# A two-layer encoder on one core: mean squares from token-major copies in the last layer, and activation halves made in two pieces

## The chip, the cores and the metric

The kernel runs on one core of one Trainium2 chip. The metric is the device time of one execution in microseconds (us), median of several runs. The engines are named as in the profile: PE is TensorE (matmuls; PEld its weight loads), DVE is VectorE, ACT is ScalarE, POOL is GpSimd, SP is SyncE, which issues most transfers. They run side by side, each in its own program order, and wait for one another by semaphores.

## The reference

512 tokens of width 1024 pass two layers in fp32. The first mixes tokens by stick-breaking attention with 16 heads, the second by a gated linear recurrence (rglru). Behind each mixer stands a squared-ReLU network of inner width 4096, and a norm ends the whole.

```python
def rms_norm(x, g):
    y = x * lax.rsqrt(jnp.mean(x * x, axis=-1, keepdims=True) + EPS)
    return y * g

def squared_relu_mlp(h, w1, w2):
    u = jax.nn.relu(h @ w1)
    return (u * u) @ w2

for layer in range(2):
    h = rms_norm(x, norm_mix[layer])
    x = x + (stick_breaking_attention(h, ...) if layer == 0 else rglru_block(h, ...))
    h = rms_norm(x, norm_mlp[layer])
    x = x + squared_relu_mlp(h, mlp_w1[layer], mlp_w2[layer])
return rms_norm(x, norm_final)
```

## The kernel before

Activations are held feature-major: 8 tiles `x[c]` of 128 features by 512 tokens. Every product is made three times over, with operands split into a high half (fp32r, a cast by ACT) and a low half (the remainder, a subtraction by DVE): high by high, high by low, low by high. So each weight slab of 128x1024 costs one cast `wh` on ACT and one subtraction `wl` on DVE, and PE multiplies with three passes.

The two networks (class `Mlp`) are computed in four quarters of the inner width. The first columns of the first matrix are plain products of 512 tokens (`product`, L236 to L238). All else is done with a 2x2 block scheme of seven products instead of eight. An "up" group takes seven products, P1 P5 P6 P3 P7 P2 P4, each of 24 matmuls of 256 columns (L1018), and gives activations `u[0]` to `u[3]`. Quarters two to four have two such groups (p = 0 and 1). The first quarter of the last layer has only group 1, since group 0 comes from four plain products. Then the "down" products of the second matrix follow, fourteen of 12 matmuls with 512 columns (L1149); their results are collected token-major in `mlp.c` (the program's names c, seen as `mlp.y(t, h)`: token tile t of 128, half h of the features).

Activations are ReLU and square, both on ACT (`u<-u`), with additions by DVE between them. Their halves for the second matrix stand in `bh` and `bl` for group 0 and in `sh` and `sl` for group 1; `split` makes them, sums of them (`sums`) follow in blocks 3 to 6. The additions on weights that the block scheme needs are made by DVE (`b<-b,b`) or by transfers that add, issued by POOL (L1094).

What order the work has: PE's order is as the program is written. Around the four quarters (`run`), ACT and DVE are `Ordered`: each instruction is told to follow the one recorded before it, so their queues stand as written, too. Each step of `run` calls `leave` for the step before: it copies or collects what that step left in PSUM, then prepares weights four steps on. Elsewhere a scheduler orders ACT, DVE and POOL by due times; SP's queue comes out of it as well.

The norm ahead of a network is applied behind it: the gain is multiplied in first, and each token's inverse mean square `rr` scales the token-major sums when they are collected (L797 with `ps,rr,c`). In the last layer `rr` comes from `Squares`: ACT squares the eight feature-major tiles (L159, L162), DVE adds them up (L164), PE sums over partitions by four products with ones (`inv_squares`, L174, of one column each), and DVE makes the inverse (L180 to L182). `transposed` has meanwhile copied `x` token-major into `mlp.c` (L1737, L1740), where the network's output is added.

At the end (`end`), DVE collects the last two products, ACT squares the tokens' rows with a running sum (`square`, L1764), `root` makes the factor, POOL multiplies some tiles with the last norm's gain ahead (`scaled`), and ACT (`one`, L1806) or DVE (`both`, L1797) scales the rows; SP stores them in the order of the program (L1788).

Of the kernel before, what the change touches and what calls it, by code (L numbers as in the profile page):

```python
# [64 lines left out]
def hybrid_encoder(  # L65
# [741 lines left out]
    class Mlp:  # L807
# [28 lines left out]
        def __init__(self, ctx, layer):  # L836
            self.layer, self.sq, self.first = layer, Squares(), None
            self.V, self.A = Ordered(V), Ordered(A)
            self.mp = ctx.enter_context(tc.tile_pool(name=f"mlp{layer}", bufs=2))
            self.c = [  # L840
                self.mp.tile([P, 2, S], F32, tag=f"c{i}", name=f"c{i}", bufs=1) for i in range(4)
            ]
            self.begun, self.a, self.next_slabs = set(), {}, []
            self.turns = count()
            self.blocks = ExitStack()
            self.bp = self.blocks.enter_context(tc.tile_pool(name=f"blocks{layer}", bufs=2))
            self.u, self.lows, self.s3, self.slots = {}, {}, [], None

            self.s41 = self.bp.tile([P, C // 2, S], F32R, tag="s41", name="s41", bufs=1)

        def y(self, t, h):
# [54 lines left out]
                    ]  # L906
            return self.a[p]

        def split(self, p, i, of, to):
            h, l = (t[:, i, to, :] for t in self.places(p))  # L910
            u = self.u[p][:, i, of, :]
            self.A.copy(h, u)
            self.ready = self.V.tensor_tensor(l, u, f(h), ALU.subtract)

        SUMS = (
            (2, 3, 2, ALU.subtract), (3, 0, 3, ALU.subtract), (0, 2, 0, ALU.subtract), (1, 0, 1, ALU.add),
# [242 lines left out]
        def run(self, first, between, end):  # L1159
# [102 lines left out]
            def leave(i):  # L1262

                if i < 0:
                    return
                kind, q4, p, name = steps[i]
                bank = sums[kind, q4, p if kind == "up" else 0][self.PRODUCTS[name][3]]
                if kind == "down":
# [39 lines left out]
                if later:  # L1308
                    later.pop()()
                prepare_or_hold(i)  # L1310
                if op:
                    def rest(u=u, at=at):
                        self.A.activation(u[at], u[at], AF.Relu)
                        self.square(u[at])
                        if p:
                            self.split_slot(p, u[at], at)

                    if p and name == "P3":
                        later.append(rest)
                    else:  # L1320
                        rest()
                    if name == "P2" and not p:
                        self.split(p, slice(0, 2), slice(0, 3), slice(0, 3))
                elif name == "P4" and p:
                    last_sums(u, self.SUMS[2:3])
                    self.split_slot(p, u[2], 5)
                    last_sums(u, self.SUMS[3:])
                    waiting[:] = [(p, u[j], 3 + j) for j in (0, 1, 3)]
                elif name == "P4":
                    self.sums(p, slice(0, 2), slice(1))  # L1330
                elif name in ("P5", "P6") and p:
                    n = ("P5", "P6").index(name)
                    if q4 + n == 0:
                        self.replace()
                    self.split(0, n, slice(0, 4), slice(3, 7))

            waiting, later, held = [], [], []
            if self.layer:
# [5 lines left out]
                self.halves_of_sums(0)  # L1344
                self.sums_of_x(2)
                self.halves_of_sums(1)
                for c in range(2):
                    self.squared(c, ps[c])
                make(0)
                add(1)  # L1350
                self.sums_of_x(3)
# [3 lines left out]
                self.halves_of_sums(3)  # L1355
                add(2)
                ps = self.product(3)
                self.rr = self.sq.inv_squares(bank("z"))
                self.squared(3, ps)
                self.split(0, slice(0, 2), slice(0, 3), slice(0, 3))  # L1360
                make(2)
                self.sums(0, slice(0, 2), slice(1))
                held.append(3)
# [32 lines left out]
                e.turn(False)  # L1396
            end([ws[len(steps) - 2 + g] for g in range(2)], sums["down", NQ - 1, 0]["X"])

        def blocks_from_the_third_slab(self, transposed, end):
            units = {("up", 0): self.from_up(0)}  # L1400

            def between():
# [5 lines left out]
                self.load(units["up", 0], (1, "b11"), (1, "b12"), (1, "b22"))  # L1408
                units["down", 0] = self.from_down(0)
                self.load(units["down", 0], (0, "b11"), (0, "b12"), (1, "b11"))  # L1410
                for n in range(C):
                    self.sq.chunk(n, x[n], e=V)
                return ps

            self.run(units, between, end)
# [311 lines left out]
    with ExitStack() as mctx:  # L1727
# [83 lines left out]
        def end(ws, xs):  # L1811
# [21 lines left out]
            for i, cols in enumerate(parts):  # L1833
                ps = mlp.bank()[:, :HS]
                for g in range(2):
                    mlp.times("P4", g, 1, ws[g], ps, True, cols)
                with tc.issue_after(scaled_two.ins) if i else nullcontext():
                    mlp.collect("P4", 1, ps, cols)
                sq = square(3, 0, 1 + i, cols, end=i == 1)
                if i == 0:  # L1840
                    scaled_two = both(2, 0, two)
                    one(2, 1, two, last=sq)
                    scaled(3, 0, cols, behind=mlp.y(2, 0))
            rt = root(3, 2)
            both(3, 0, rt, parts[1])
            one(3, 1, rt)
# [72 lines left out]
```

## Time and profile before

| | |
|---|---|
| median of 3 runs (lowest, highest) | 1025.52 us (1024.94, 1025.79) |
| profiled execution, its own time | 1025.03 us |
| its span, first to last instruction | 1022.8 us |
| mean granted TensorE clock | 0.998 |
| PE busy | 1014.2 us, 99% |
| DVE busy | 866.3 us, 85% |
| ACT busy | 708.9 us, 69% |
| POOL busy | 176.3 us, 17% |
| last layer's up and down products, and the end | from 726.3 us on |

Times in rows count from the start of the span. A row of the timeline has start, length, engine, line, operation, output and inputs, shapes, count, and in brackets how long the engine idled before it and what ended that. A row of groups has count, busy time and mean length in ns, then idle time ahead. L797 is a helper through which all `Ordered` instructions go, so such rows are told apart by their tiles. Matmuls overlap: successive starts tell their spacing, not their length.

### The profile page before, as it was taken

What the parts mean: (1) busy time and instruction counts of PE and PEld (TensorE: products, weight loads), DVE (VectorE), ACT (ScalarE), POOL (GpSimd) and SP (SyncE); (2) the same over time, 40 slices, a digit from 0 to 9 for tenths busy, and PEclk for the clock granted to TensorE, in tenths of its full rate; (3) what the DMA queues carried; (4) which work ended last, traced back from release to release, by engine and by line L of the source; (5) the groups of instructions that cost most, each with busy time, mean ns of one, the idle gap of its engine ahead of it and who ended that gap; (6) DMA issues with size and microseconds to landing.
All of it is one profiled execution on the core that took longest, in us unless ns stands there. A gap on an engine that the chain in (4) does not pass through costs nothing.

```text
span 1022.8 us, 16121 instructions
## 1 busy us (share of the span) xinstructions
PE 1014.2 (99%) x5962; PEld 893.6 (87%) x5962; DVE 866.3 (85%) x1159; ACT 708.9 (69%) x1094; POOL 176.3 (17%) x241
## 2 busy tenths in 40 slices
PE   9999999999999999999999999999999999999997
PEld 7988888888888988988988888888988988988986
DVE  7978787848789898898899888986898898898897
ACT  7777676836766863863875799966873763873865
POOL 0454444420010010010011121200010010010013
PEclk9999999999999999999999999999999999999999
DMA  7745454527536667667682575452467667667653
GB/s 238 237 105 147 126 148 100 161 94 290 137 78 200 179 146 203 170 144 204 175 209 81 149 189 157 104 206 83 97 138 202 165 144 201 174 142 203 173 114 106
DMA packets 53550, 161.53 MB, mean 158 GB/s; under 512 B 6752, under 2 KB 8288, under 8 KB 53472
## 3 DMA queue, kind: packets, MB, share of 16 engines
q1 hardware_dynamic: 42240, 120.48, 35.6%
q0 software_dynamic: 10944, 39.85, 22.8%
q8 instruction: 47, 0.77, 0.3%
q14 instruction: 31, 0.25, 0.1%
q10 hardware_dynamic: 288, 0.18, 0.1%
HBM read 138.46 MB, written 4.19 MB: 139 GB/s over the span
## 4 chain that ended last, share of the span: by engine, by line
PE 94%; DVE 3%; ACT 2%; DMA 1%; issue 1%; SPq 0%; DVEq 0%; ACTq 0%
PE ps_t L1149 16%; PE ps_acc L1018 9%; PE ps_acc L1149 8%; PE ps_z L1018 8%; PE ps_acc L236 5%; PE ps_acc L238 5%; PE ps_acc L237 5%; PE ps_o L1018 5%; PE ps_z L1149 4%; PE ps_t L236 2%; PE ps_t L237 2%; PE ps_t L238 2%; PE ps_t L636 2%; PE ps_o L236 2%; PE ps_o L237 2%; PE ps_o L238 2%
## 5 line engine op out<-in xcount | busy, mean ns | idle before, releaser
L797 ACT CAST wh<-b 128x1024 fp32r<-128x1024 f32 x174 | 180.6, 1050 | 119.8 <-DVE b L797 81.0
L797 DVE TENSOR_TENSOR wl<-b,wh 128x1024 fp32r<-128x1024 f32 x174 | 210.3, 1218 | 39.9 <-ACT wh L797 38.4
L1094 POOL DMA_DIRECT2D b<-in_w_dn x40 | 34.9, 873 | 292.8 <-DVE b L797 196.7
L236 PE MATMUL ps_acc<-xgh,wh 128*128 128x512 f32 x192 | 78.3, 408 | 0.0
L238 PE MATMUL ps_acc<-xgl,wh 128*128 128x512 f32 x192 | 75.2, 391 | 0.0
L237 PE MATMUL ps_acc<-xgh,wl 128*128 128x512 f32 x192 | 75.1, 391 | 0.0
L1094 POOL DMA_DIRECT2D b<-in_w_up x26 | 22.6, 869 | 297.2 <-DMA b<-in_w_up 80.9
L797 ACT ACTIVATE u<-u 128x512 f32<-128x512 f32 x103 | 65.0, 632 | 12.3 <-DVE u L797 10.4
L614 DVE TENSOR_TENSOR_SCAN scan<-keep,later 128x128 f32<-128x128 f32 (+1 forms) x64 | 58.2, 913 | 16.4 <-ACT keep L604 10.4
L618 POOL TENSOR_TENSOR w<-w,scan 128x128 f32<-128x128 f32 (+1 forms) x64 | 53.4, 836 | 55.4 <-DVE scan L614 50.2
L797 DVE TENSOR_TENSOR b<-b,b 128x1024 f32<-128x1024 f32 x50 | 61.1, 1222 | 1.3
L231 DVE TENSOR_TENSOR wl<-raw,wh 128x512 fp32r<-128x512 f32 (+2 forms) x66 | 57.1, 893 | 5.6 <-ACT wh L229 5.6
L229 ACT CAST wh<-raw 128x512 fp32r<-128x512 f32 (+2 forms) x66 | 46.5, 742 | 21.3 <-PE ps_acc L238 7.3
L797 DVE TENSOR_TENSOR u<-u 128x512 f32<-128x512 f32 (+1 forms) x85 | 54.2, 638 | 4.1 <-ACT u L797 2.3
L797 ACT CAST wh<-raw 128x1024 fp32r<-128x1024 f32 x47 | 49.0, 1048 | 3.2 <-PE ps_acc L1149 3.1
L1018 PE MATMUL ps_z<-xgh,wh 128*128 128x256 f32 x216 | 50.7, 277 | 0.0
L1149 PE MATMUL ps_t<-wh,sl 128*128 128x512 f32 x120 | 46.9, 391 | 0.2 <-DVE sl L797 0.2
L1149 PE MATMUL ps_t<-wh,bl 128*128 128x512 f32 x120 | 46.8, 390 | 0.0
L1149 PE MATMUL ps_t<-wh,sh 128*128 128x512 f32 x120 | 46.8, 390 | 0.0
L1149 PE MATMUL ps_t<-wh,bh 128*128 128x512 f32 x120 | 46.8, 390 | 0.0
L797 DVE TENSOR_TENSOR wl<-raw,wh 128x1024 fp32r<-128x1024 f32 x37 | 45.5, 1229 | 1.1 <-ACT wh L797 1.1
L1018 PE MATMUL ps_acc<-low,wh 128*128 128x256 f32 x192 | 44.7, 276 | 0.0
(423 smaller groups left out, 3209.9 us busy)
## 6 DMA issues: line engine op xcount, KB each, us to landing
b<-in_w_dn SPq DMA_DIRECT2D x48, 512.0 KB, 4.1
b<-in_w_dn POOLq DMA_DIRECT2D x40, 512.0 KB, 5.5
b<-in_w_up SPq DMA_DIRECT2D x39, 512.0 KB, 4.4
b<-in_w_up POOLq DMA_DIRECT2D x26, 512.0 KB, 5.4
raw<-in_w_dn SPq DMA_DIRECT2D x16, 512.0 KB, 4.5
raw<-in_w_in SPq DMA_DIRECT2D x16, 512.0 KB, 3.7
raw<-in_w_up SPq DMA_DIRECT2D x13, 512.0 KB, 4.2
raw<-in_w_qk SPq DMA_DIRECT2D x12, 512.0 KB, 3.8
```

What stands on the lines that cost most here:

```text
L229: A.copy(wh[:, k, :], raw[:, k, :])
L231: V.tensor_tensor(wl[:, k, :], raw[:, k, :], f(wh[:, k, :]), ALU.subtract)
L236: PE.matmul(ps, wh, ah, start=start, stop=False)
L237: PE.matmul(ps, wl, ah, start=False, stop=False)
L238: PE.matmul(ps, wh, al, start=False, stop=stop)
L614: V.tensor_tensor_scan(sc[:, S - n : S][:, ::-1], keep[:, :n][:, ::-1], later[:, S - n :][:, ::-1], 1.0, ALU.mult, ALU.max,)
L618: G.tensor_tensor(wt, wt, sc[:, S - n + 1 : S + 1], ALU.mult)
L636: PE.transpose(tr[:, (qb - kb) * P : (qb - kb + 1) * P], w[pair, j, qb][:, kb * P : (kb + 1) * P], ident,)
L797: ins = getattr(self.e, name)(*args, **kwargs)
L1018: PE.matmul(ps[:, i * HS : (i + 1) * HS], m, y, start=new and i == k == low == 0 and y is h, stop=(low, i, k) == steps[-1], skip_group_che ...
L1094: G.dma_start(out=unit[b].rearrange("p j n -> p (j n)"), in_=unit["src"](to), accum_op=ALU.add)
L1149: PE.matmul(sums[to][i], m, y[:, j, :], start=new and g == j == low == 0 and m is h, stop=g == low == j == 1, skip_group_check=not new,)
```

## The change

1. In the last layer the eight feature-major squares, their sum, the four products with ones and DVE's three small operations go. Instead ACT squares the eight token-major tiles `mlp.y(t, h)` with an accumulator (`squares_of_tokens`): two tiles behind `halves_of_sums(1)`, two behind the fourth plain product (both pairs with a PSUM bank for the unused output), one each behind the first and the fourth up product, two behind the second down product (unused output in SBUF). There `inv_squares_of_tokens` makes `rr` with POOL, DVE (reciprocal) and POOL. The old `leave` is renamed `left`, and a new `leave` calls it first.
2. In the last layer's first quarter, the halves of group 0 are made in two pieces: for i = 0 behind the first two plain products, for i = 1 behind the fourth.
3. In quarters two to four of both layers, the halves of group 0's `u[1]` and `u[2]` are made ahead (high halves behind P7, low halves behind P2's addition) and those of `u[0]` alone behind P2.
4. At the end the collection of tile (3, 0)'s second half no longer stands behind the scaling of tile (2, 0): that scaling now follows the last collection, and POOL's last product with the gain does not wait for it either.

```diff
+            self.ss = spare[:, 8:].rearrange("p (h t) -> p h t", h=2)
...
-        def split(self, p, i, of, to):
+        def split(self, *which):
+            self.high_halves(*which)
+            self.low_halves(*which)
+
+        def high_halves(self, p, i, of, to):
+            self.A.copy(self.places(p)[0][:, i, to, :], self.u[p][:, i, of, :])
+
+        def low_halves(self, p, i, of, to):
             h, l = (t[:, i, to, :] for t in self.places(p))
-            u = self.u[p][:, i, of, :]
-            self.A.copy(h, u)
-            self.ready = self.V.tensor_tensor(l, u, f(h), ALU.subtract)
+            self.ready = self.V.tensor_tensor(l, self.u[p][:, i, of, :], f(h), ALU.subtract)
...
+                left(i)
+                if self.layer and i < 10 and place(i) in (7, 10, 15):
+                    ts = {7: ((2, 0),), 10: ((3, 0),), 15: ((2, 1), (3, 1))}[place(i)]
+                    junk = home.tile([P, S], F32, tag="osum", name="junk", bufs=1)
+                    self.squares_of_tokens(junk, *ts)
+                    if place(i) == 15:
+                        self.inv_squares_of_tokens()
...
                 prepare_or_hold(i)
+                if name == "P2" and not p:
+                    self.low_halves(0, slice(0, 2), slice(1, 3), slice(1, 3))
...
+                    if name == "P7" and not p:
+                        self.high_halves(0, slice(0, 2), slice(1, 3), slice(1, 3))
                     if name == "P2" and not p:
-                        self.split(p, slice(0, 2), slice(0, 3), slice(0, 3))
+                        self.split(p, slice(0, 2), slice(0, 1), slice(0, 1))
...
                 self.halves_of_sums(1)
+                self.squares_of_tokens(bank("t"), (0, 0), (1, 0))
                 for c in range(2):
                     self.squared(c, ps[c])
+                self.split(0, 0, slice(0, 3), slice(0, 3))
                 make(0)
...
                 ps = self.product(3)
-                self.rr = self.sq.inv_squares(bank("z"))
+                self.squares_of_tokens(bank("t"), (0, 1), (1, 1))
                 self.squared(3, ps)
-                self.split(0, slice(0, 2), slice(0, 3), slice(0, 3))
+                self.split(0, 1, slice(0, 3), slice(0, 3))
...
+        def squares_of_tokens(self, junk, *tiles):
+            for t, h in tiles:
+                self.A.activation(
+                    junk, self.y(t, h), AF.Square, accum_out=self.ss[:, h, t : t + 1]
+                )
+
+        def inv_squares_of_tokens(self):
+            rr = self.rr = small.tile([P, 2 * NB], F32, tag="rr", name="rr")
+            G.tensor_tensor(rr[:, :NB], self.ss[:, 0, :], self.ss[:, 1, :], ALU.add)
+            G.tensor_scalar(rr[:, :NB], rr[:, :NB], 1.0 / D, EPS, ALU.mult, ALU.add)
+            self.V.reciprocal(rr[:, :NB], rr[:, :NB])
+            G.tensor_scalar(rr[:, NB:], rr[:, :NB], -1.0, None, ALU.mult)
...
-                for n in range(C):
-                    self.sq.chunk(n, x[n], e=V)
...
-                with tc.issue_after(scaled_two.ins) if i else nullcontext():
-                    mlp.collect("P4", 1, ps, cols)
+                mlp.collect("P4", 1, ps, cols)
                 sq = square(3, 0, 1 + i, cols, end=i == 1)
                 if i == 0:
-                    scaled_two = both(2, 0, two)
                     one(2, 1, two, last=sq)
-                    scaled(3, 0, cols, behind=mlp.y(2, 0))
+                    scaled(3, 0, cols)
+            both(2, 0, two, last=mlp.gained)
```

How this stands in the engines' queues, at three places. First ACT around the fourth plain product of the last layer (`u<-ps_acc` takes that product, `bh<-u` are the halves of group 0, `wh` weights), before:

```order
L797 CAST s_7404<-x 128x512
L797 ACTIVATE u<-ps_acc 128x512
L797 ACTIVATE u<-u 128x512
L797 CAST bh<-u 128x2x768
L797 CAST wh<-b_7531 128x1024
L797 COPY u<-ps_z 128x512
L797 CAST wh<-b_7535 128x1024
```

and now:

```order
L797 CAST s_7410<-x 128x512
L797 ACTIVATE ps_t,eps_t<-c_7404 128x512 x2
L797 ACTIVATE u<-ps_acc 128x512
L797 ACTIVATE u<-u 128x512
L797 CAST bh<-u 128x768
L797 CAST wh<-b_7537 128x1024
L797 COPY u<-ps_z 128x512
L797 CAST wh<-b_7541 128x1024
L797 ACTIVATE junk,eps_t<-c_7405 128x512
```

Two squares stand ahead of the fourth product's activation, half of the split has left this place (it stands ahead of the first up weights now), and one square follows the second of the weights.

Second, ACT in the second quarter of the last layer, around P2 of group 0, before:

```order
L797 ACTIVATE u<-u 128x2x256 x2
L797 CAST wh<-b_8120 128x1024
L797 ACTIVATE u<-u 128x2x256 x2
L797 CAST bh<-u 128x2x768
L797 ACTIVATE u<-ps_acc 128x2x256
L797 ACTIVATE u<-u 128x2x256
L797 COPY u<-ps_z 128x512
L797 CAST wh<-b_8176 128x1024
```

and now:

```order
L797 ACTIVATE u<-u 128x2x256 x2
L797 CAST bh<-u 128x2x512
L797 CAST wh<-b_8114 128x1024
L797 ACTIVATE u<-u 128x2x256 x2
L797 CAST bh<-u 128x2x256
L797 ACTIVATE u<-ps_acc 128x2x256
L797 ACTIVATE u<-u 128x2x256
L797 COPY u<-ps_z 128x512
L797 CAST wh<-b_8170 128x1024
```

Two thirds of the halves have moved ahead of a weight's cast and of P2's activation; one third stands where all stood. On DVE the two low halves, of 1024 and 512 elements, stand together where the one of 1536 stood, behind the weight's subtraction.

Third, DVE at the end (the products `ps_o` and `ps_t` of 256 columns are the two last collections, `c_7399` and later `c_7405` tiles 2 and 3 of half 0), before:

```order
L797 SCALAR_TENSOR_TENSOR c_7399<-ps_o,rr,c_7399 128x256
L1784 RECIPROCAL rt<-rt 128x1
L1797 SCALAR_TENSOR_TENSOR c_7399<-c_7399,rt,gb 128x512
L797 SCALAR_TENSOR_TENSOR c_7399<-ps_t,rr,c_7399 128x256
L1784 RECIPROCAL rt<-rt 128x1
L1797 SCALAR_TENSOR_TENSOR c_7399<-c_7399,rt,gb 128x256
```

and now:

```order
L797 SCALAR_TENSOR_TENSOR c_7405<-ps_o,rr,c_7405 128x256
L1818 RECIPROCAL rt<-rt 128x1
L797 SCALAR_TENSOR_TENSOR c_7405<-ps_t,rr,c_7405 128x256
L1831 SCALAR_TENSOR_TENSOR c_7405<-c_7405,rt,gb 128x512
L1818 RECIPROCAL rt<-rt 128x1
L1831 SCALAR_TENSOR_TENSOR c_7405<-c_7405,rt,gb 128x256
```

The last collection and the scaling of 512 columns have changed places. SP's stores keep their order: tile (2, 0), (2, 1), then the three of tile 3.

Between the last layer's two weight subtractions and the first collection, DVE's queue has the new reciprocal; in POOL's queue the addition and the scaling for the mean stand together ahead of a transfer that adds, and the negation behind it.

More of the change, by code (lines that the diff above doesn't have):

```diff
@@ L1265, in leave, with left @@
                     return
+                left(i)
[5 more added lines that the diff above has]
+                        self.inv_squares_of_tokens()
+            def left(i):
                 kind, q4, p, name = steps[i]
```

## The prediction

> **What bounds the kernel now.** I read the page's busy row and its chain of waits first, then TensorE's own waits, then stage by stage how long equal work takes.
>
> ```profile
> span 1022.8 us, 16121 instructions
> PE 1014.2 (99%) x5962; PEld 893.6 (87%) x5962; DVE 866.3 (85%) x1159; ACT 708.9 (69%) x1094; POOL 176.3 (17%) x241
> PE 94%; DVE 3%; ACT 2%; DMA 1%; issue 1%; SPq 0%; DVEq 0%; ACTq 0%
> PE ps_t L1149 <- DVE sl L797: 0.2, 1, 0.2
> ```
>
> TensorE (PE) bounds it: 94% of the chain that ends last, and apart from its start only one recorded wait, 0.2 us. What can be won is therefore small and of three kinds: matmuls that disappear, matmuls spaced wider than elsewhere, and the tail after PE. The last two do not show as waits; they show as equal work that takes unequal time. The first row below, of a table of stretches, holds the seven up products of the last layer's first quarter, 168 matmuls of 256 columns (L1018 alone; the columns are length, PE, PEld, clock, DMA share, GB/s). The next two hold the up and the first down products of its quarters two and three, the same instructions in both (length, PE, PEld, DVE, ACT, POOL, then the same). The last two are of the chain: the first five products of quarter three, and one that follows.
>
> ```profile
> 727.13:747.16 20.03, 20.03 (x168) 19.83 (x168) 1.00 0.51 137
> 785.27:829.96 44.69, 44.47 (x362) 42.96 (x361) 36.09 (x37) 33.06 (x46) 4.61 (x6) 1.00 0.65 155
> 862.82:906.52 43.70, 43.70 (x362) 42.72 (x361) 36.19 (x37) 33.66 (x46) 4.72 (x6) 1.00 0.65 159
> 862.82 13.75 PE ps_acc L1018 x120
> 876.58 2.72 PE ps_z L1018 x24
> ```
>
> Seven products of the third quarter take 13.75 + 2 x 2.72 = 19.19 us; those of the first lose 20.03 - 19.19 = 0.84 us. The second quarter loses 44.69 - 43.70 = 0.99 us against its twin. The granted clock is 1.00 in all of them. These are the places where an edit can pay.
>
> **Part one: the sums of squares leave PE.** Ahead of the first losing stretch stand the four one-column products of the squares with the ones, two passes each. The last row is the seventh up product behind them.
>
> ```profile
> 726.32 0.95 PE L174 MATMUL ps_z<-ones,ssq 128*128 128x1 f32 x8
> 727.13 0.36 PE L1018 MATMUL ps_z<-xgh,wh 128*128 128x256 f32 x1
> 744.34 2.83 PE ps_z L1018 x24
> ```
>
> They go: 727.13 - 726.32 = **0.81 us**, certain on PE. The next term is less so. Behind them every product takes 2.83 us to the last, 118 ns a matmul; in the third quarter, where 512-column matmuls stand ahead, 2.72 us, 113 ns. In the changed order the up products follow 512-column matmuls directly, so I take the third quarter's spacing: **0.84 us**. Its bounds are 0 (the slow spacing stays) and 20.03 - 7 x 2.72 = 0.99.
>
> The work moves to ScalarE (ACT) and, in tiny pieces, to GpSimd (POOL). The eight feature-major squares and seven DVE additions lie beside the last mixer's output products, where PE has no gap: their removal wins nothing. The eight new squares are priced by the end's squares, which have an accumulator and its readout too.
>
> ```profile
> L1764 ACT ACTIVATE junk<-c 128x512 f32<-128x512 f32 x7 | 4.4, 626 | 3.4 <-DVE c L797 3.4
> L797 ACT CAST sh<-u 128x512 fp32r<-128x512 f32 x49 | 30.3, 618 | 0.7
> L1764 ACT ACTIVATION_READ_ACCUMULATOR junk<-c 128x1 f32 x9 | 1.7, 186 | 0.0
> L797 ACT CAST bh<-u 128x768 fp32r<-128x768 f32 x2 | 1.7, 840 | 0.0
> L797 ACT CAST bh<-u 128x1024 fp32r<-128x1024 f32 x16 | 16.8, 1050 | 5.2 <-DVE u L797 5.2
> 714.96 0.60 ACT L797 ACTIVATE u<-ps_z 128x512 f32<-128x512 f32 x1 [1.47 <-PE ps_z L238]
> 726.52 0.60 ACT L797 ACTIVATE u<-ps_acc 128x512 f32<-128x512 f32 x1 [2.33 <-PE ps_acc L238]
> 727.81 1.48 ACT L797 CAST bh<-u 128x1536 fp32r<-128x1536 f32 x1
> 729.33 1.76 DVE L797 TENSOR_TENSOR bl<-u,bh 128x1536 fp32r<-128x1536 f32 x1 [1.09 <-ACT bh L797]
> 731.00 1.22 DVE L797 TENSOR_TENSOR wl<-b,wh 128x1024 fp32r<-128x1024 f32 x1
> 751.44 0.68 DVE L797 TENSOR_TENSOR sl<-u,sh 128x512 fp32r<-128x512 f32 x1
> 752.70 0.39 PE L1149 MATMUL ps_t<-wh,sl 128*128 128x512 f32 x1
> ```
>
> A pair costs 2 x 0.63 + 0.19 = 1.45 us. The first pair falls into ACT's wait of 1.47 us, the second into that of 2.33 us, which the early half split (0.84 us, about 0.8 in a row) has cut to about 1.5; both fit, barely. The next two squares come singly into an ACT that follows PE by several us, the last two ahead of ACT's longest pause of the down stretch.
>
> Does ACT and DVE's chain keep up with a PE that is 0.81 + 0.84 = 1.65 us early at 752.70? Of the large split of 1536 elements half is now made ahead. Behind the fourth product ACT needs 0.84 instead of 1.48 us, and DVE about half of 1.76 us. So DVE begins the next weight's low half about 0.64 + 0.8 = **1.4 us earlier** than 731.00, if it is free by then: its own early half makes it some 0.8 us late, which its wait of 1.09 us and the three little operations on the mean, which go, take up. From there DVE is hardly idle up to the low half that PE waits for (ends 751.44 + 0.68 = 752.12, wanted at 752.70, slack 0.58). Then the slack is 0.58 + 1.4 - 1.65 = 0.33 us: PE keeps its gain. If DVE came less than 1.65 - 0.58 = 1.07 us earlier, the difference would be given back there.
>
> **Part two: halves made ahead.** In each quarter with a first group the split of three activations (1536 elements) becomes two (1024) ahead and one (512) behind the last. ACT pays 1.05 + 0.62 for 1.48, DVE 1.22 + 0.68 for 1.76 us, more in sum, but at another time. In the second quarter of the last layer, the only one that loses time:
>
> ```profile
> 804.32 1.05 ACT L797 CAST wh<-b 128x1024 fp32r<-128x1024 f32 x1 [1.41 <-DVE b L797]
> 806.60 1.48 ACT L797 CAST bh<-u 128x1536 fp32r<-128x1536 f32 x1
> 809.15 0.57 ACT L797 COPY u<-ps_z 128x512 f32<-128x512 f32 x1
> 808.12 1.76 DVE L797 TENSOR_TENSOR bl<-u,bh 128x1536 fp32r<-128x1536 f32 x1 [1.49 <-ACT bh L797]
> 810.70 1.22 DVE L797 TENSOR_TENSOR wl<-b,wh 128x1024 fp32r<-128x1024 f32 x1
> 809.77 0.39 PE L1018 MATMUL ps_z<-bh,wh 128*128 128x256 f32 x1
> 829.96 0.50 PE L1149 MATMUL ps_t<-wh,sl 128*128 128x512 f32 x1 [0.22 <-DVE sl L797]
> ```
>
> ACT waits 1.41 us before the cast at 804.32: the new high halves (1.05) fit there. The low halves (1.22) fit DVE's wait of 1.49 us. Behind the last activation ACT then has 0.62 instead of 1.48 us, so the copy at 809.15, after which PE's accumulation at 809.77 may begin, and the next cast come about 0.85 us earlier. DVE's chain from 810.70 to the low half of 829.96, which has hardly a pause, moves by as much, less a few hand-offs. It starts at one of PE's own products, so it keeps the 1.65 us of part one too. I take **0.75 us** of the 0.99; bounds 0 (the extra piece costs what it frees) and 0.99. In the five other quarters the same pauses hide it and there is no loss to win: 0. Without those pauses the extra work would be 0.19 us of ACT in each.
>
> **Part three: the end.** The last collection no longer stands behind the scaling of the third tile.
>
> ```profile
> 1014.84 1.28 POOL L797 TENSOR_TENSOR c<-c,gb 128x512 f32<-128x512 f32 x1
> 1013.89 0.74 DVE L1797 SCALAR_TENSOR_TENSOR c<-c,rt,gb 128x512 f32<-128x512 f32 x1
> 1015.29 1.37 DVE L1797 SCALAR_TENSOR_TENSOR c<-c,rt,gb 128x512 f32<-128x512 f32 x1
> 1016.59 0.47 DVE L797 SCALAR_TENSOR_TENSOR c<-ps_t,rr,c 128x256 f32<-128x256 f32 x1
> 1017.09 0.42 ACT L1764 ACTIVATE junk<-c 128x256 f32<-128x256 f32 x1 [0.58 <-DVE c L797]
> GB/s 0 0 0 41 393 401 213 0 66 410 393 393 418 393 369 426 279 0 0 0 0 0 344 401 402 426 410 115 0 0 324 201 377 410 361 373 53 0 0 0
> ```
>
> The last row is what the stores moved from 1012 to 1022, in slices of 0.25 us. The collection waits for PE alone and can start about 0.6 us earlier, near 1016.0 (an estimate); the square behind it, and what follows to the last store, can come some 0.5 us earlier. But the moved scaling now ends at 1016.0 + 0.47 + 0.74 = 1017.2, or at 1017.6 if POOL slows it by part of the 0.63 us that the 1.37 us are over 0.74, where it ended at 1015.29 + 1.37 = 1016.66. SyncE sends the stores in program order, so two of 256 KB stand behind it, and with the last three a megabyte: at 400 GB/s 2.6 us. Their bytes move from 1017.5 now, 0.85 us after that scaling's end. That gives an end at 1020.7 to 1021.1, against about 1021.2 now. I take **0.1 us**; bounds -0.2 and +0.5. The Trainium skill, GPSIMD Engine Reference, "8. Key points", says that GpSimd contends with VectorE instructions that have two SBUF inputs; the pair of 1.37 beside 0.74 us agrees. By that rule the moved scaling pays again, beside POOL's last product, and this part is worth 0.1 us; without it 0.5.
>
> **The sum.** 0.81 + 0.84 + 0.75 + 0.1 = 2.5 us. The profiled execution took 1025.03 us, 2.23 around its span, and stands 0.49 below the median 1025.52. So 1022.5 for its like and **1023.0 us** for the median.
>
> **The rivals.** *The slow spacing stays.* What keeps it is not shown. The stretch from 727 is slow throughout and others recover, which speaks for the entry; that no row names the mechanism speaks against. Then 0.84 falls away: 1023.9. The Trainium skill, TensorE: Matmul & The Clock Gate, "Back-to-back issue gap", has the spacing set by weight load and matmul together; by it what came before would not matter, and this rival holds.
> *The gain is given back at 752.70.* If ACT does not hold the first two pairs in its pauses (1.45 in 1.47), DVE comes no earlier and PE waits 1.07 us: 1023.0 + 1.07 = 1024.1.
> *The split frees nothing.* 1023.0 + 0.75 = 1023.8. The pauses of 1.41 and 1.49 us speak against.
> *Slower: DVE blocked by the reciprocal.* The mean square's reciprocal stands on DVE ahead of the first collection and waits for two POOL operations, which wait for ACT's last squares.
>
> ```profile
> 753.63 2.00 ACT L797 CAST wh<-b 128x1024 fp32r<-128x1024 f32 x2
> 756.58 2.35 DVE L797 TENSOR_TENSOR wl<-b,wh 128x1024 fp32r<-128x1024 f32 x2
> L618 POOL TENSOR_TENSOR w<-w,scan 128x128 f32<-128x128 f32 x16 | 7.1, 441 | 6.9 <-DVE scan L614 6.4
> ```
>
> In the old times the casts end at 755.6, the squares 1.45 us later at 757.1, two POOL operations of at most 0.44 us (the nearest row has 128 elements, these have 4) at 758.0; DVE gets there at 756.58 + 2.35 = 758.9. Hidden by 0.9 us. Queued behind the reciprocal are the collections, an addition of weights and the low halves that PE wants next. So POOL would have to take at least 0.9 + 2.5 = 3.4 us longer before the whole is slower; at 6 us longer it is 1023.0 + 6 - 0.9 = 1028.1. POOL's queue holds no transfer between the two operations, which speaks against.
>
> **How the numbers follow.** Forecast 0.50, of which four fifths below 1023.47; slow spacing 0.15; given back 0.14; split frees nothing 0.08; slower 0.06; more than the sum (0.5 in part three, 0.99 in part two) 0.07, at 1022.4. What a measurement of this kernel can tell from no change is 0.2%, 2.05 us, so faster means under 1023.47 and slower over 1027.57. Faster: 0.40 from the forecast, 0.07 from more than the sum, 0.10 from the three cases at 1023.8 to 1024.1, about a quarter of which scatter brings below that line: 0.57. Slower 0.06; the rest, 0.37, is within. Range 1021.7 (the upper bounds together, 0.81 + 0.99 + 0.99 + 0.5 = 3.3, and 0.5 of scatter) to 1024.8 (little more than the 0.81 holds).
>
> **What would show it.** Right: no L174 row in the last layer; the seven up products in 19.2 us; no gap at the first product with sl; the second quarter's up stretch at 43.9 to 44.0 us; DVE's reciprocal without idle time before it. Wrong: products of 2.83 us throughout, a wait for sl of about 1 us in the first quarter, 44.7 us in the second, or a last store landing later after PE's last matmul than now.

## The result, and the profile after

| | before | changed |
|---|---|---|
| median (lowest to highest) | 1025.41 us (1024.80 to 1026.56), 15 runs | 1023.32 us (1022.84 to 1024.84), 15 runs |
| ratio, 95% interval | | 0.9979 (0.9972 to 0.9986) |
| profiled execution, its span | 1025.03, 1022.8 us | 1023.33, 1021.0 us |

The changed kernel is 2.1 us faster, 0.21%, at the edge of what a measurement of this kernel can tell; the whole interval, 0.14% to 0.28%, lies on the faster side. The forecast was 1023.0 us. That the total came out does not mean that its terms did: the largest, 0.84 us, gave 0.09, and gains that had been put at zero made up for more than half of what was missed.

The page of the changed kernel, span, busy time and shares of the chain:

```profile
span 1021.0 us, 16117 instructions
PE 1012.2 (99%) x5954; PEld 892.3 (87%) x5954; DVE 862.2 (84%) x1157; ACT 710.9 (70%) x1109; POOL 178.3 (17%) x243
PE 98%; DMA 0%; ACT 0%; DVE 0%; issue 0%; POOL 0%; SPq 0%; DVEq 0%; ACTq 0%
```

TensorE now has 98% of the chain where it had 94%. Its work shrank by eight matmuls, and the pieces of ScalarE and VectorE that stood in the chain are out of it.

The chain of waits, the first and the last of the seven up products of the last layer's first quarter, then the opening five products of its second and third quarters and one that follows:

```profile
726.77 2.83 PE ps_z L1024 x24
743.73 2.83 PE ps_z L1024 x24
784.69 13.75 PE ps_acc L1024 x120
861.39 13.75 PE ps_acc L1024 x120
875.14 2.72 PE ps_z L1024 x24
```

The first quarter's products still take 2.83 us each, as before, though no one-column product stands ahead of them any more. The second and third quarters, by stretches as in the prediction (length, PE, PEld, DVE, ACT, POOL, clock, DMA share, GB/s):

```profile
784.66:828.53 43.87, 43.87 (x363) 42.62 (x361) 36.08 (x38) 33.64 (x46) 4.60 (x6) 1.00 0.66 159
861.39:905.09 43.70, 43.70 (x362) 42.74 (x361) 36.94 (x40) 34.29 (x47) 5.21 (x6) 1.00 0.66 162
```

The second quarter took 44.69 us and takes 43.87; its twin is unchanged at 43.70.

To see where the time went I matched the matmuls of the two traces one by one (the eight removed ones left out) and took how much earlier each starts. Profiled executions differ by more than 1 us in when transfers land up to 202 us, ahead of anything that an edit touches; so every column is less the kernel's own shift at 202.05 us. Negative is earlier than before, in us. The last column is the time from the last matmul's start to the end of the span, 7.23 us before.

| kernel | 479.09, layer 0, last quarter | 727.13, first up product | 752.70, first with sl | 785.22, second quarter | 829.96, its down products | 939.11, last quarter | last matmul | tail |
|---|---|---|---|---|---|---|---|---|
| changed | -0.20 | -1.09 | -1.18 | -1.15 | -2.00 | -2.11 | -2.16 | 7.09 |
| changed, again | -0.20 | -1.09 | -1.17 | -1.17 | -2.03 | -2.13 | -2.19 | 7.10 |
| squares alone | +0.32 | -0.47 | -0.55 | -0.55 | -0.56 | -0.57 | -0.60 | 7.52 |
| halves ahead alone | -0.20 | -0.28 | -0.28 | -0.28 | -1.13 | -1.23 | -1.28 | 7.25 |
| end alone | +0.13 | +0.13 | +0.12 | +0.13 | +0.13 | +0.10 | +0.07 | 7.09 |
| changed, first opening at 36 | -0.34 | -1.22 | -1.90 | -1.62 | -2.48 | -2.59 | -2.65 | 7.10 |
| changed, three POOL products | -0.20 | -1.09 | -1.17 | +3.63 | +2.77 | +2.68 | +2.63 | 7.38 |

A row is best read from one of its columns to the next. Where an edit touches nothing, traces still differ by up to 0.3 us: the squares alone lose 0.32 us in layer 0 and 0.29 in the tail, the end alone loses 0.13 in layer 0, and 0.15 of the 0.34 that the opening at 36 gains there came at 208 us, far ahead of what it changes.

So the change is worth 2.16 + 0.14 = 2.30 us in these traces: 0.28 in layer 0 (0.08 of it behind 479.09), 0.81 by the one-column products, 0.09 at the first up product behind them, nothing from the spacing, 0.85 in the second quarter, 0.16 behind it, 0.14 at the end; 0.03 are lost again in the rest of the first quarter, in the first trace alone.

ScalarE and VectorE in the second quarter, where the halves moved:

```profile
802.36 1.05 ACT L797 CAST bh<-u 128x1024 fp32r<-128x1024 f32 x1
803.74 1.05 ACT L797 CAST wh<-b 128x1024 fp32r<-128x1024 f32 x1 [0.32 <-DVE b L797]
806.02 0.62 ACT L797 CAST bh<-u 128x512 fp32r<-128x512 f32 x1
805.97 1.82 DVE L797 TENSOR_TENSOR bl<-u,bh 128x1024 fp32r<-128x1024 f32 x2
```

The new cast of 1.05 us fills what was ScalarE's wait of 1.41 us ahead of the cast at 804.32 and leaves 0.32; behind the last activation 0.62 us stand where 1.48 stood; both low halves run in one piece without VectorE's wait of 1.49 us.

The place of the reciprocal, VectorE's rows and then POOL's:

```profile
755.47 2.35 DVE L797 TENSOR_TENSOR wl<-b,wh 128x1024 fp32r<-128x1024 f32 x2
758.20 0.18 DVE L797 RECIPROCAL rr<-rr 128x4 f32<-128x4 f32 x1 [0.38 <-POOL rr L1431]
755.97 1.91 POOL L1430 TENSOR_TENSOR rr<-eps_t 128x4 f32<-128x4 f32 x1 [4.30 <-ACT junk L797]
757.97 0.19 POOL L1431 TENSOR_SCALAR rr<-rr 128x4 f32<-128x4 f32 x1
```

POOL's addition of four elements a row took 1.91 us, and VectorE stood idle for 0.38 us ahead of the reciprocal. TensorE hardly felt it in this kernel (the 0.03 us above). In the second trace of the same kernel, at the same place, VectorE did not wait at all:

```profile
757.69 0.18 DVE L797 RECIPROCAL rr<-rr 128x4 f32<-128x4 f32 x1
755.76 0.77 POOL L1430 TENSOR_TENSOR rr<-eps_t 128x4 f32<-128x4 f32 x1 [4.29 <-ACT junk L797]
756.62 1.04 POOL L1431 TENSOR_SCALAR rr<-rr 128x4 f32<-128x4 f32 x1
```

Of the ten traces that have this reciprocal with nothing added ahead of it, three show the wait of 0.38 us and seven none.

The end: ScalarE's scaling of tile (2, 1), VectorE's moved scaling of tile (2, 0), POOL's last products, and what the stores moved from 1010 to 1020 us in slices of 0.25 us:

```profile
1014.22 0.71 ACT L1840 ACTIVATE c<-c,rt 128x512 f32<-128x512 f32 x1
1014.66 1.11 DVE L1831 SCALAR_TENSOR_TENSOR c<-c,rt,gb 128x512 f32<-128x512 f32 x1
1013.25 1.96 POOL L797 TENSOR_TENSOR c<-c,gb 128x512 f32<-128x512 f32 x2
GB/s 0 0 0 0 0 172 401 401 74 0 213 393 418 426 410 320 418 426 123 0 0 0 0 0 0 0 172 410 393 410 401 381 385 414 418 369 385 58 0 0
```

VectorE's scaling begins beside POOL's last product and takes 1.11 us where 0.74 is its time alone. The stores pause from 1014.75 to 1016.5 us and then move the last megabyte.

### The profile page after: what moved, and what is told of

It is laid out like the page before. It is cut to its first block, busy times and chain, and to the rows that moved or that the text cites. A ratio compares the mean times of both kernels' runs of the same rounds, so it can differ in the third digit from the quotient of the medians.

```text
span 1021.0 us, 16117 instructions
## 1 busy us (share of the span) xinstructions
PE 1012.2 (99%) x5954; PEld 892.3 (87%) x5954; DVE 862.2 (84%) x1157; ACT 710.9 (70%) x1109; POOL 178.3 (17%) x243
## 4 chain that ended last, share of the span: by engine, by line
PE 98%; DMA 0%; ACT 0%; DVE 0%; issue 0%; POOL 0%; SPq 0%; DVEq 0%; ACTq 0%
PE ps_t L1155 16%; PE ps_acc L1024 10%; PE ps_z L1024 9%; PE ps_acc L1155 9%; PE ps_o L1024 6%; PE ps_acc L236 5%; PE ps_acc L238 5%; PE ps_acc L237 5%; PE ps_z L1155 4%; PE ps_t L236 2%; PE ps_t L237 2%; PE ps_t L238 2%; PE ps_t L636 2%; PE ps_o L236 2%; PE ps_o L238 2%; PE ps_o L237 2%
```

## The experiments

### The parts apart

The first question was whether the terms belong to the parts to which the forecast gave them: above all, whether the second quarter's loss goes because TensorE is earlier (part one) or because of the halves (part two). Three kernels are the kernel before with one part of the diff each.

The squares alone:

```diff
+ self.squares_of_tokens(bank("t"), (0, 0), (1, 0))
+ self.split(0, 0, slice(0, 3), slice(0, 3))
...
- self.rr = self.sq.inv_squares(bank("z"))
+ self.squares_of_tokens(bank("t"), (0, 1), (1, 1))
- self.split(0, slice(0, 2), slice(0, 3), slice(0, 3))
+ self.split(0, 1, slice(0, 3), slice(0, 3))
...
- for n in range(C):
-     self.sq.chunk(n, x[n], e=V)
```

> The kernel before with the first part alone: sums of squares from token-major copies, and the first quarter's halves of group 0 in two pieces; neither the halves ahead in the later quarters nor the new end. If the parts add up, PE wins the one-column products (0.81 us and 0.08 us at the entry) and no more: 0.9 us in all, about 1024.5, products of 2.83 us in the last layer's first quarter, and the second quarter's stretch loses its 0.99 us as before (44.7 us). If instead the second quarter's loss came from the squares' place (a late start of ACT and DVE), it is gone here too: 43.9 us and about 1023.7.

Measured: 1024.89 us, ratio 0.9987 (0.9978 to 0.9995), beside a kernel before of 1026.02. Stretches of the second quarter and of its twin, then rows of the chain in the first and in the second:

```profile
784.68:829.36 44.68, 44.35 (x362) 42.75 (x361) 36.08 (x37) 33.01 (x46) 4.60 (x6) 1.00 0.66 153
862.23:905.93 43.70, 43.70 (x361) 42.72 (x361) 36.20 (x38) 33.42 (x46) 4.74 (x6) 1.00 0.69 161
743.75 2.83 PE ps_z L1024 x24
806.01 1.48 ACT bh L797
809.12 0.96 ACT wh L797
810.11 1.23 DVE wl L797
```

TensorE gains 0.79 us between 479 us and the first up product and keeps it. The spacing stays at 2.83 us: the one-column products were not its cause. The second quarter still takes 44.68 us, and the cast of 1.48 us, of all three activations at once, stands in the chain. So the earlier start does not mend the second quarter, nor does it harm it.

The halves alone:

```diff
+ if name == "P2" and not p:
+     self.low_halves(0, slice(0, 2), slice(1, 3), slice(1, 3))
+ if name == "P7" and not p:
+     self.high_halves(0, slice(0, 2), slice(1, 3), slice(1, 3))
- self.split(p, slice(0, 2), slice(0, 3), slice(0, 3))
+ self.split(p, slice(0, 2), slice(0, 1), slice(0, 1))
```

> The kernel before with the halves made ahead in quarters two to four alone. Theory: the second quarter of the last layer goes from 44.69 to about 43.9 us, and the small waits in the other quarters (0.26 us in the first layer, 0.17 us behind) go too: 1.2 us in all, about 1024.2. Rival: only together with the first part, which brings ACT and DVE earlier: then under 0.3 us, about 1025.2.

Measured: 1024.21 us, ratio 0.9983 (0.9974 to 0.9992). The second quarter's stretch:

```profile
785.86:829.69 43.83, 43.83 (x361) 42.58 (x360) 36.08 (x38) 33.28 (x46) 4.60 (x6) 1.00 0.68 157
```

43.83 us with the one-column products still in place. The second quarter's 0.85 us belong to the halves alone, whatever comes ahead. The matched starts show two more gains that I had put at zero: 0.28 us in layer 0, most of it in four steps at 384, 448, 523 and 536 us, and 0.15 behind the second quarter, at 920, 922 and 984. All kernels with the halves show these steps; the two without show no gain in layer 0. Together the halves are worth 1.28 us, more than the squares.

The end alone:

```diff
- with tc.issue_after(scaled_two.ins) if i else nullcontext():
-     mlp.collect("P4", 1, ps, cols)
+ mlp.collect("P4", 1, ps, cols)
...
-         scaled_two = both(2, 0, two)
-         scaled(3, 0, cols, behind=mlp.y(2, 0))
+         scaled(3, 0, cols)
+ both(2, 0, two, last=mlp.gained)
```

> The kernel before with the new end alone. From the pair of profiles 0.2 us (from PE's last matmul to the end 7.27 us before, 7.06 us after), about 1025.2; nothing else moves. If the late store of tile (2, 0) costs what the collection wins: 0.0.

Measured: 1025.41 us, ratio 0.9992 (0.9983 to 1.0001), which does not exclude nothing. In the table the kernels with this part have a tail of 7.09 or 7.10 us, but for one of 7.38; without it there are 7.23, 7.25 and 7.52. That would be 0.14 us or a little more, but a tail with the same end scatters by more than that (7.23 and 7.52 us without the part, 7.09 and 7.38 with it): the gain is likely, not shown.

The medians cannot split the parts. By them the three gain 1.13, 1.81 and 0.61 us, together 3.55, where the whole gained 2.09, and 2.61 when it ran again; so the parts are told apart by the matched traces, one for each.

### Why the first quarter's products are wide apart

With the one-column products excluded, I looked at the starts of all up products. In every quarter that opens with product P1 of group 0, the first 24 matmuls come 118 to 120 ns apart and all behind at 113 ns. Only the last layer's first quarter, which opens with P1 of group 1, stays at 118 ns for all 168. One thing in which the code treats the two apart is an offset. Each half of the weights lies in a buffer with 64 elements of room a row (`ROOM`). Weights of up products start 16 elements into it (`UP_AT`), but those of P1 of group 0 start at 36 (`OPEN_AT`). Three kernels move that start; no byte that is computed changes.

First, the changed kernel with the last layer's very first up product at 36 too:

```diff
- at = self.OPEN_AT if (p, name) == (0, "P1") else UP_AT
+ at = self.OPEN_AT if i == 0 or (p, name) == (0, "P1") else UP_AT
```

> The changed kernel, with the weights of the last layer's very first up product 36 elements into their buffer instead of 16, as the opening product of every later quarter has it; nothing else moves. Theory of the place: those opening products are the only 24 matmuls of their quarters at 118 to 120 ns, all behind them run at 113 ns; so here 24 matmuls at about 119 and 144 at 113 ns, 19.2 instead of 19.86 us, and about 0.6 us less than the changed kernel: 1022.7. Rival: the spacing comes from what stands ahead (plain products with other operands): 2.83 us throughout, 1023.3.

Measured: 1022.78 us, ratio 0.9963 (0.9951 to 0.9976). The chain, first, second and last of the seven:

```profile
725.86 2.87 PE ps_z L1024 x24
728.73 2.73 PE ps_o L1024 x24
742.34 2.72 PE ps_z L1024 x24
```

Only the first product's weights moved, and the six behind it, untouched, take 2.72 us in place of 2.83. By the table TensorE gains 0.68 - 0.09 = 0.59 us over the changed kernel up to 752.70, and gives 0.28 back before 785.22.

Second, the changed kernel with every opening product at 16:

```diff
- at = self.OPEN_AT if (p, name) == (0, "P1") else UP_AT
+ at = UP_AT
```

> The changed kernel with the opening up product of every quarter at offset 16 of its weight buffer, where the others lie, in place of 36. If the offset of the opening weights decides the spacing, the up products of every quarter keep 118 ns a matmul to the last: some 312 matmuls of a quarter lose 4.5 ns each, 1.4 us a quarter, in six quarters 8.4 us, so about 1031.7 us where the changed kernel takes 1023.3. If the first quarter of the last layer is slow for what stands ahead of it, the six quarters stay at 113 ns and the time stays at 1023.3 us.

Measured: 1031.18 us, ratio 1.0051 (1.0035 to 1.0066), slower than the kernel before. The chain in the third quarter of the last layer:

```profile
866.77 14.13 PE ps_acc L1024 x120
880.90 2.83 PE ps_z L1024 x24
```

2.83 us throughout, 118 ns a matmul, in all six other quarters. Third, the opposite, all up products at 36:

```diff
- ROOM, UP_AT, V_AT = 64, 16, 48
+ ROOM, UP_AT, V_AT = 64, 36, 48
```

> The changed kernel with all up products' weights at offset 36, the opening ones and the others. If a change of offset within the quarter is what makes the products quick, no quarter has one now and all stay at 118 ns: about 1.4 us in each of six quarters, 1031.7 us. If offset 36 of the opening product alone makes the quarter quick, whatever follows, the six quarters stay at 113 ns and the first of the last layer too gets quick, because it now opens at 36: 1022.7 us.

Measured: 1035.65 us, ratio 1.0098 (1.0084 to 1.0112). The same two rows:

```profile
868.93 14.39 PE ps_acc L1024 x120
883.31 2.88 PE ps_z L1024 x24
```

2.88 us, 120 ns, and no quarter recovers. So neither 16 nor 36 is the quick offset. A quarter is quick if its opening weights lie at 36 and the others at 16; with one offset for all it is slow, at 118 or 120 ns. Other pairs of offsets, 16 and then 36 among them, were not run. The theory's direction was right and its size too small (1031.7 us expected), as it had 118 ns for both. What in TensorE or its reads of the weights carries the effect of the first product over hundreds of later ones is not shown by any row, and I leave it open.

The Trainium skill, TensorE: Matmul & The Clock Gate, "Back-to-back issue gap", has the spacing set by weight load and matmul together. Here the same loads and matmuls, at the same offset of 16, come 113 or 118 ns apart by what opened the quarter, so that rule does not cover this.

### The order of the last stores

The fourth tile of the end, (2, 1), is ready at 1014.22 + 0.71 = 1014.93 us, before the third, (2, 0), whose moved scaling ends at 1014.66 + 1.11 = 1015.77. Yet no byte moves from 1014.75 to 1016.5 us: its store stands behind that one's in SyncE's queue, although the changed program names it first (SyncE's queue comes out of the scheduler). The changed kernel with the two stores exchanged:

```diff
- store(t, h, cols)
+ with tc.issue_after(sent.ins) if sent else nullcontext():
+     store(t, h, cols)
...
- one(2, 1, two, last=sq)
+ sent = one(2, 1, two, last=sq)
...
- both(2, 0, two, last=mlp.gained)
+ both(2, 0, two, last=mlp.gained, sent=sent)
```

> The changed kernel with the store of the fourth tile of the end issued ahead of that of the third. The fourth is ready first and its store waits in SyncE's order behind the third's. If that order is what the end still loses, the stores' bytes fill the hole from 1014.8 to 1016.5 us, the last megabyte ends about 0.4 us earlier and the time is 1022.9 us. If the last tile's own work sets the end, nothing moves: 1023.3 us.

Measured: 1022.22 us, ratio 0.9965 (0.9952 to 0.9977). To tell fractions of a microsecond apart it ran once more beside the changed kernel itself:

> The changed kernel itself, once more, beside the next three on one chip, so that fractions of a microsecond can be told apart. Every theory: 0.9979 of the kernel before, 1023.3 us where that takes 1025.4.

> The changed kernel with the fourth tile's store ahead of the third's, once more, beside the changed kernel. The end after TensorE's last matmul was 6.6 instead of 7.06 us in one profile. If that is the whole of it: 0.45 us less than the changed kernel on the same chip.

Measured on that chip: the changed kernel 1023.09 us, ratio 0.9978 (0.9968 to 0.9988); with the stores exchanged 1022.42, 0.9970 (0.9960 to 0.9981). The stores from 1010 to 1020 us in the latter:

```profile
GB/s 0 0 0 213 401 401 33 0 303 393 402 393 401 377 401 401 74 0 0 0 8 401 401 238 238 418 381 369 226 385 393 373 348 17 0 0 0 0 0 0
```

The pause shrank from seven empty slices, 1.75 us, to three. The tail is 6.57 us in both traces, against 7.09 and 7.10: 0.5 us, and 0.67 by the medians. So half a microsecond of the end that the change left was the order of two stores.

### Both together

```diff
- at = self.OPEN_AT if (p, name) == (0, "P1") else UP_AT
+ at = self.OPEN_AT if i == 0 or (p, name) == (0, "P1") else UP_AT
...
- both(2, 0, two, last=mlp.gained)
+ both(2, 0, two, last=mlp.gained, sent=sent)
```

> The changed kernel with both: the opening product of the last layer's first quarter at offset 36 and the fourth tile's store ahead of the third's. The two are at different ends of the layer and add up: 0.6 + 0.4 us less than the changed kernel, 1022.3 us. If the store's order is worth nothing, 1022.7 us, as the offset alone.

> Opening offset 36 in the last layer's first quarter and the fourth tile's store first, once more, beside the changed kernel. If the products' gain of 0.6 us is kept behind the quarter: 0.45 + 0.6, so 1.0 us less than the changed kernel. If VectorE, late by the reciprocal's wait, takes most of it back at its collections around 763 to 766 us, as one profile of it shows (0.4 to 0.5 us): 0.6 us less, no better than the store's order alone by more than 0.2 us.

Measured: 1022.60 us, ratio 0.9968 (0.9957 to 0.9980), and 1022.28, 0.9969 (0.9957 to 0.9980). That beats the kernel before and the changed one, but the exchange of stores alone gave 1022.22 and 1022.42: the two cannot be told apart. The repeat's two theories stay open: it gained 0.81 us on the changed kernel, between the 1.0 of the first and the 0.6 of the second, and 0.14 on the stores' order alone. Up to 752.70 the two traces gain 1.78 and 1.79 us (counted as in the table), 0.6 more than the changed kernel, but at 785.22 only 1.19 and 1.50 are left. VectorE and POOL around the reciprocal, in the first trace (two rows) and in the second (three):

```profile
758.06 0.18 DVE L797 RECIPROCAL rr<-rr 128x4 f32<-128x4 f32 x1 [0.38 <-POOL rr L1431]
755.97 1.78 POOL L1430 TENSOR_TENSOR rr<-eps_t 128x4 f32<-128x4 f32 x1 [4.43 <-ACT junk L797]
```

```profile
757.90 0.18 DVE L797 RECIPROCAL rr<-rr 128x4 f32<-128x4 f32 x1
755.96 0.77 POOL L1430 TENSOR_TENSOR rr<-eps_t 128x4 f32<-128x4 f32 x1 [4.29 <-ACT junk L797]
756.83 1.04 POOL L1431 TENSOR_SCALAR rr<-rr 128x4 f32<-128x4 f32 x1
```

With VectorE's wait of 0.38 us 0.59 is given back, without it 0.29; the kernel with the offset alone, which has no such wait either, gives back 0.28. So the forecast's rival of a gain given back to VectorE is real, at 766 us instead of 752.70, and appears only once the spacing is won.

### The price of a late reciprocal

The changed kernel with three more POOL products of 128x512 between the last square and the mean:

```diff
- G.tensor_tensor(rr[:, :NB], self.ss[:, 0, :], self.ss[:, 1, :], ALU.add)
+ for _ in range(3):
+     block = G.tensor_tensor(junk, junk, junk, ALU.mult)
+ with tc.issue_after(block.ins):
+     G.tensor_tensor(rr[:, :NB], self.ss[:, 0, :], self.ss[:, 1, :], ALU.add)
```

> The changed kernel with three more products of 128x512 on GpSimd between the last square and the mean of the squares, which VectorE's reciprocal waits for; the output is the same. It prices the slower rival. The changed kernel's reciprocal already waits 0.4 us. Three products of 1.3 to 2 us hold it 4 to 6 us longer, unless GpSimd stood idle before; VectorE's low halves behind it come as much later. If nothing else covers that, TensorE waits for a low half of the next weights or activations some 3 to 5 us and the time is 1026.3 to 1028.3 us. If the weights ahead and the pauses behind cover it, under 1 us: at most 1024.3 us.

Measured: 1027.74 us, ratio 1.0019 (1.0010 to 1.0028). POOL's first two products, VectorE's reciprocal, TensorE's wait, and two stretches (clock in the third column from the right):

```profile
755.41 3.58 POOL L1431 TENSOR_TENSOR junk<-junk 128x512 f32<-128x512 f32 x2 [4.30 <-ACT junk L797]
761.37 0.18 DVE L797 RECIPROCAL rr<-rr 128x4 f32<-128x4 f32 x1 [3.27 <-POOL rr L1434]
PE ps_t L1155 <- DVE c L797: 2.9, 1, 2.9
759.40:762.54 3.14, 0.20 (x1) 0.03 (x1) 1.07 (x3) 0.00 (x0) 2.08 (x5) 0.99 0.62 86
762.54:766.00 3.46, 3.46 (x8) 2.76 (x9) 2.89 (x4) 1.72 (x2) 0.00 (x0) 0.52 0.37 73
```

Against the changed kernel, and less the shift at 202.05 us (0.57 there, -0.02 here), the reciprocal is 761.37 - 758.20 + 0.59 = 3.8 us later. TensorE then loses 3.63 + 1.15 = 4.8 us, more than the delay. It waits 2.9 us at a down product, for a collection queued behind the reciprocal; and then the granted clock is 0.52 for 3.46 us, in which eight matmuls start 425 ns apart instead of 226: 8 x 0.2 = 1.6 us. The time lies in the upper part of the first theory's range, but for another reason: TensorE waited for the collection, not for a low half, and the clock was not in the theory. (Part of the delay is a transfer that POOL issued between the second and the third product, at 758.94 us.)

## Why the prediction was right or wrong

**What bounds it.** Right: TensorE, in small pieces, and 2.30 us were to be had where 2.5 were forecast.

**One-column products, 0.81 us.** Right: by the matched starts the changed kernel gains 0.89 us between 479 and 727 us, of which the halves alone give 0.08, so 0.81 are left; the squares alone bring 0.79. ScalarE and VectorE take nothing of it back.

**Spacing, 0.84 us.** Wrong, and this is the step that failed: "In the changed order the up products follow 512-column matmuls directly, so I take the third quarter's spacing". The neighbour in time was taken for the cause because it was the one difference that the rows showed. The cause is where the opening product's weights lie, taken together with where the others' lie: the kernels with the first opening at 36, with 16 throughout and with 36 throughout show it. What the step did deliver is 0.09 us at the first product, the wide start of 727.13. The rival "the slow spacing stays" was true, and its 1023.9 was its price with all else as forecast.

**No give-back at 752.70.** Right, and close to its numbers. VectorE's next low half began at 730.03, 0.97 us earlier on the trace's own clock. The changed trace runs 0.57 us late from 202.05 us on, and 0.28 of the gain is layer 0's; so part one brought it 0.97 + 0.57 - 0.28 = 1.26 us, where 1.4 were forecast and 1.07 named as the limit. The limit itself was set too high, since it counted the spacing's 0.84, which did not come. The low half for the down product now ends at 750.31 + 0.68 = 750.99 and is wanted at 752.09, with a slack of 1.10 us where 0.58 were:

```profile
730.03 1.23 DVE L797 TENSOR_TENSOR wl<-b,wh 128x1024 fp32r<-128x1024 f32 x1
750.31 0.68 DVE L797 TENSOR_TENSOR sl<-u,sh 128x512 fp32r<-128x512 f32 x1
752.09 0.39 PE L1155 MATMUL ps_t<-wh,sl 128*128 128x512 f32 x1
```

**Halves ahead, 0.75 us in the second quarter.** Right: 0.85, from the halves alone. "In the five other quarters the same pauses hide it and there is no loss to win: 0" was wrong: 0.28 in layer 0 and 0.15 to 0.16 behind the second quarter, which the halves alone show too. Those quarters had losses, steps of 0.02 to 0.10 us each, below what the view of waits lists; I had compared two quarters, not six.

**The end, 0.1 us.** Measured 0.14, the right size but within the scatter of the tail. The moved scaling paid 0.37 us beside POOL (1.11 for 0.74), as the choice between 0.1 and 0.5 assumed; the rule weighed there (the Trainium skill, GPSIMD Engine Reference, "8. Key points") agrees with that row. That a reversed order of two stores would free 0.5 us more was not seen, though the text named the queue.

**The reciprocal.** The cover of 0.9 us was mis-sized: "two POOL operations of at most 0.44 us (the nearest row has 128 elements, these have 4)" took 1.91 and 0.19 us, as the add ends with VectorE's pair of subtractions (755.97 + 1.91 = 757.88; 755.47 + 2.35 = 757.82). It ate the cover and 0.38 us more. In the second trace the two took 0.77 and 1.04 us: about all of the cover, and no more. So the sign of being right, a reciprocal without idle time before it, came in seven traces of ten. The place and the kind of the rival's mechanism were right: delayed by 3.8 us, it makes the kernel slower than before. Its price was too low: it counted as loss the time that VectorE waits at the reciprocal, which was 3.27 us there, and 4.8 were lost; the clock was not in the sum.

**The sum.** In place of 0.81 + 0.84 + 0.75 + 0.1 = 2.5 stand 0.28 + 0.81 + 0.09 + 0.85 + 0.16 + 0.14 = 2.33, less 0.03. That the time came so near was luck: of the 0.75 us missed in one term, 0.28 + 0.16 = 0.44 were found in the quarters put at zero.

## What to carry to other kernels

When equal work takes unequal time, list every stretch of it, not the slow and one quick one, and look at what they share: here six quarters against one named the offset of one weight buffer, where a comparison of two named the wrong cause. A tiny operation on GpSimd is priced by what VectorE runs beside it, not by its size. Where a stall of about 3 us is added to a busy TensorE, price the slower clock behind it too, and look at the order of the last stores before the work that feeds them.

## What the runs showed of the hardware

- Matmuls of 256 columns in fp32r came 113, 118 or 120 ns apart at a granted clock of 1.00, by the offset of the weights in their buffers and by that of the product that opened the quarter: 36 then 16, 113 ns; 16 throughout, 118; 36 throughout, 120. Over all quarters that is 8 to 13 us (1031.2 and 1035.7 beside 1023.1). The mechanism is open.
- An addition of 128x4 on POOL took 0.76 to 0.77 us in seven traces and 1.78 to 1.91 us in three. In all ten it began while VectorE ran the first of two subtractions with two inputs from SBUF, back to back; it ended 0.06 us behind the first of them in the seven, and 0.06 us behind the second in the three. The Trainium skill, SBUF — State Buffer, "Terms", says that the port pair that VectorE and GpSimd share is locked for a full instruction, and that the loser blocks fully. The traces agree: the addition waits out a whole subtraction, or both, and does not merely slow down.
- A TensorE wait of 2.9 us, in a kernel with a granted clock of 1.00 before it, was followed by 3.46 us at 0.52, in one trace. The Trainium skill, TensorE: Matmul & The Clock Gate, "What's actually happening", has half the clock behind an idle window of about 3.4 us; here 2.9 us sufficed.
